# Depthwise convolution of 31 taps: from taps shared by three engines to products of shifted copies on the matrix engine

## The chip, the cores and the metric

The kernel runs on one core of a Trainium2 chip. The metric is the device time of one execution in microseconds (us). The engines are named as in the profile: PE is the matrix engine (PEld its weight loads), DVE the vector engine, ACT the scalar engine, POOL the general engine, SP the engine that issues the DMAs. All engines of the core run at the same time; each takes its own instructions strictly in the order in which they were written down, and semaphores make one wait for another.

## What is computed

The reference is a chain of layers on a sequence of 512 tokens with 1024 features, all in float32. The change touches one of them, the "conformer" layer, and in it one line: a causal convolution over time, for each feature by itself, with 31 taps.

```python
def causal_dwconv(x, w):              # x (1, 512, 1024), w (31, 1024)
    k_w = w.shape[0]
    return lax.conv_general_dilated(
        x, w[:, None, :].astype(x.dtype), window_strides=(1,), padding=[(k_w - 1, 0)],
        dimension_numbers=('NWC', 'WIO', 'NWC'), feature_group_count=x.shape[-1])

def conformer_conv(h, w_in, b_in, dw, dw_b, ln_g, ln_b, w_out, b_out):
    D = h.shape[-1]
    u = h @ w_in + b_in
    u = u[..., :D] * jax.nn.sigmoid(u[..., D:])
    u = causal_dwconv(u, dw) + dw_b
    u = jax.nn.silu(layernorm(u, ln_g, ln_b))
    return u @ w_out + b_out
```

So the output at time t is the sum over the lags d = 0 to 30 of the input at t - d times the tap of lag d of that feature. Before this layer stands a feed-forward layer (`ffn`, layer 0), behind it a cross attention (`xattn`, layer 1), whose keys and values are worked out from another input, `mem`, of 256 tokens.

## The kernel before

**Layout.** Features lie on the 128 partitions, in 8 chunks j = 0 to 7; the 512 tokens lie along the free dimension. A tile of one chunk is 128x512 in float32.

**Dense products.** `linear` (L222) takes weight tiles of 128 input rows by 1024 values. Each is loaded from DRAM by a DMA that SP issues into one of two raw buffers (`wr`, L51), and is split into a high part (ACT, L63) and a low part (DVE or POOL, L64), for which there are three buffers each. `acc3` (L212) then makes each product of three fast matmuls (L218 to L220). The weights `kv_k1` and `kv_v1` are not split: they are used from the raw buffer, in one plain float32 matmul (L216). A plain float32 matmul is two records of PE in the trace, each with a weight load of its own.

**The conformer layer (L576).** For each chunk j, `lin([j])` makes two output tiles (the gate and the value, 48 fast matmuls together); `evict` (L621) scales them by the norm's factor on DVE, takes the sigmoid on ACT and writes `us[j]` on DVE (L629). Then `conv(j)` (L590) writes `ys[j]`, and `add(j)` (L618) adds the mean over the features, by a plain float32 product, into a PSUM bank `sums` that collects over all chunks. The loop at L636 issues, for each j: `lin([j + 2])`, one eighth of the attention's keys (`next(keys)`, 8 plain float32 matmuls of 256 columns), `conv(j)`, `add(j - 1)`. `memory` (called at L634) prepares the input for the keys. Behind the loop come the last `add`, the layer norm over the features, which can start only when all eight chunks are in `sums`, and the attention's values (L216 again), put into the gaps of the layer norm by `fill`.

**`conv(j)` before.** The 31 lags are cut in three, by the table `TAPS`. The first `npe` lags (25 over all chunks) are products on PE with a diagonal matrix `dg`, which ACT makes (L598, L599). The last 8 to 14 lags (100 in all) are a multiplication on ACT into `cq` (L605, L608) and an addition on POOL (L609). The lags between them (123 in all) are fused multiply-adds on DVE into `ys[j]` (L611, L613). Two more DVE instructions (L614, L615) join the three sums and the bias.

**The order.** The program is written down with its dependencies, and a planner puts the instructions of each engine in an order: it goes through a model of the run, takes what is ready there, and among that what was written first. Buffers that are used in turn are waited for in the same way. The order that comes out is fixed; at run time an instruction that has to wait holds up all behind it on its engine, the DMAs on SP included.

Of the kernel before, what the change touches and what calls it, by code (L numbers as in the profile page):

```python
# [8 lines left out]
F32 = mybir.dt.float32  # L9
F32R = mybir.dt.float32r  # L10
AF = mybir.ActivationFunctionType
ALU = mybir.AluOpType
# [3 lines left out]
P = 128  # L16
T = 512
D = 1024
KD = D // P
# [76 lines left out]
class Net:  # L96
# [472 lines left out]

            self.linear(f"xattn_w_o{l}", KD, list(range(KD)), lambda k: o[k], out)  # L570


    KEYS = (0, 1, 2, 3, 4, 5, 6, 7)
    TAPS = [(2, 14), (1, 12), (1, 14), (1, 14), (1, 14), (1, 12), (6, 12), (12, 8)]

    def conformer(self, l, g_next):  # L576

        nc = self.nc
        self.logs = False
        rs = self.norm_done(1e-6)  # L580
        xs, side = self.xs, self.side
        ys, us, gate = {}, {}, {}
        ctx = ExitStack()
        mp = ctx.enter_context(self.tc.tile_pool(name=f"mn{l}", bufs=1, reuse_waits="tile"))
        tp = ctx.enter_context(self.tc.tile_pool(name="cz", bufs=1, reuse_waits="tile"))
        mean = tp.tile([P, P], F32, name="mean")
        nc.gpsimd.memset(mean, 1.0 / D)
        sums = self.aux()

        def conv(j):  # L590
            u = us[j]
            w = lambda d: self.vec("conv_dw", 31 * j + 30 - d)
            y = self.slot(1 - side, "h", j)
            npe, npo = self.TAPS[j]
            ps = self.aux()
            for d in range(npe):
                dg = tp.tile([P, P], F32, tag="dg", bufs=3, name=self.nm("dg"))
                nc.scalar.activation(out=dg, in_=self.ident, func=AF.Copy, scale=w(d))  # L598
                nc.tensor.matmul(ps[:, d:], lhsT=dg, rhs=u[:, : T - d], start=(d == 0), stop=(d == npe - 1), skip_group_check=True)  # L599
            z = tp.tile([P, T], F32, tag="cz", bufs=5, name=self.nm("cz"))  # L600
            d0 = 31 - npo
            for d in range(d0, 31):
                if d == d0:
                    nc.gpsimd.memset(z[:, :d], 0.0)
                    nc.scalar.activation(out=z[:, d:], in_=u[:, : T - d], func=AF.Copy, scale=w(d))  # L605
                else:
                    q = tp.tile([P, T], F32, tag="cq", bufs=2, name=self.nm("cq"))
                    nc.scalar.activation(out=q[:, d:], in_=u[:, : T - d], func=AF.Copy, scale=w(d))  # L608
                    nc.gpsimd.tensor_tensor(out=z[:, d:], in0=z[:, d:], in1=q[:, d:], op=ALU.add)  # L609
            nc.vector.memset(y[:, :npe], 0.0)  # L610
            nc.vector.tensor_scalar(out=y[:, npe:], in0=u[:, : T - npe], scalar1=w(npe), scalar2=None, op0=ALU.mult)  # L611
            for d in range(npe + 1, d0):
                nc.vector.scalar_tensor_tensor(out=y[:, d:], in0=u[:, : T - d], scalar=w(d), in1=y[:, d:], op0=ALU.mult, op1=ALU.add)  # L613
            nc.vector.tensor_tensor(out=y, in0=y, in1=z, op=ALU.add)  # L614
            nc.vector.scalar_tensor_tensor(out=y, in0=ps, scalar=self.vec("conv_dw_b", j), in1=y, op0=ALU.add, op1=ALU.add)  # L615
            ys[j] = y

        def add(j, x):  # L618
            self.last_sum = nc.tensor.matmul(sums, lhsT=mean, rhs=x, start=(j == 0), stop=(j == KD - 1))

        def evict(m, ps):  # L621
            u = self.t512("u", 3)
            nc.vector.tensor_tensor(out=u, in0=ps, in1=rs, op=ALU.mult)  # L623
            if m >= KD:
                nc.scalar.activation(out=u, in_=u, func=AF.Sigmoid, bias=self.vec("conv_b_in", m))
                gate[m - KD] = u
            else:
                us[m] = self.slot(1 - side, "l", m)
                nc.vector.scalar_tensor_tensor(out=us[m], in0=u, scalar=self.vec("conv_b_in", m), in1=gate.pop(m), op0=ALU.add, op1=ALU.mult)  # L629

        keys = self.memory_keys(l)
        lin = lambda js: self.linear("conv_w_in", KD, [m for j in js for m in (KD + j, j)], lambda k: xs[k], evict, group=2)
        lin([0])
        self.memory(mp, False)  # L634
        lin([1])
        for j in range(KD):  # L636
            if j < 6:
                lin([j + 2])
            if j in self.KEYS:
                km = next(keys)  # L640
            conv(j)
            if j:
                add(j - 1, ys[j - 1])
        for km in keys:
            pass
        values = self.memory_values(l)
        vm = next(values)

        def fill(n, after):
            with self.tc.issue_after(after.ins):  # L650
                for _ in range(n):
                    next(values)

        fill(FILL[0], self.last_sum)
        add(KD - 1, ys[KD - 1])
        fill(FILL[1], self.last_sum)
        for j in range(KD):
            nc.vector.tensor_tensor(out=ys[j], in0=ys[j], in1=sums, op=ALU.subtract)
        ps = self.aux()
        for j in range(KD):  # L660
            s = self.t512("sq", 2) if j else self.t512("acc", 1)
            nc.scalar.activation(out=s, in_=ys[j], func=AF.Square)
            if j:
                nc.vector.tensor_tensor(out=acc, in0=acc, in1=s, op=ALU.add)
            else:
                acc = s
        for b in range(4):
            last = nc.tensor.matmul(ps[:, b : b + 1], lhsT=acc[:, b * P : (b + 1) * P], rhs=self.ones[:, 0:1], start=True, stop=True)
        fill(FILL[2], last)
        v = self.small(4, "rq")  # L670
        nc.vector.tensor_scalar(out=v, in0=ps[:, :4], scalar1=1.0 / D, scalar2=1e-5, op0=ALU.mult, op1=ALU.add)
        r = self.small(4, "rq")
        self.rsqrt(r, v, 4)
        b = self.bcast_tokens(r)
        fill(FILL[3], self.last_bcast)
        ctx.close()
        zs, done = [], []
        for j in range(KD):
            y = ys[j]
            with self.tc.issue_after(done[-2]) if j > 1 else nullcontext():  # L680
                nc.vector.tensor_tensor(out=y, in0=y, in1=b, op=ALU.mult)
            self.last_silu = nc.scalar.activation(out=y, in_=y, func=AF.Silu, scale=self.vec("conv_ln_g", j), bias=self.vec("conv_ln_b", j)).ins
            hi, lo = self.pair(side, j)
            done.append(self.split(hi, lo, y).ins)
            zs.append((hi, lo))
        self.next_norm(g_next, 1 - side)

        def out(m, ps):
            nc.vector.scalar_tensor_tensor(out=self.x[m], in0=ps, scalar=self.vec("conv_b_out", m), in1=self.x[m], op0=ALU.add, op1=ALU.add)
            self.norm_chunk(m)  # L690

        self.linear("conv_w_out", KD, list(range(KD)), lambda k: zs[k], out)
        return km, vm
# [888 lines left out]
def lay_w(w):  # L1582
    k, m = w.shape
    return w.reshape(k // P, P, m // P, P).transpose(2, 1, 0, 3)


def lay_n(w):

    k, m = w.shape
    return w.reshape(k // 256, 2, P, m // 512, 512).transpose(3, 0, 2, 1, 4).reshape(-1, P, 2, 512)  # L1590
# [113 lines left out]
def by_feature(x):  # L1704
    return x.T.reshape(KD, P, -1).transpose(1, 0, 2)


def arrays(a):

    vl = vec_list(a)  # L1710
    out = {"x": by_feature(a["x"][0]), "mem": by_feature(a["mem"][0]), "vecs": np.concatenate([v for _, v in vl], axis=1)}
    out.update(rw_arrays(a))
    out.update(hy_arrays(a))
    for l in range(2):
        kv = a["xattn_w_kv"][l]
        out[f"kv_k{l}"], out[f"kv_v{l}"] = lay_w(kv[:, :D]), lay_n(kv[:, D:])
        out[f"xattn_w_q{l}"], out[f"xattn_w_o{l}"] = lay_w(a["xattn_w_q"][l]), lay_w(a["xattn_w_o"][l])
        out[f"ffn_w_in{l}"], out[f"ffn_w_out{l}"] = lay_w(a["ffn_w_in"][l]), lay_w(a["ffn_w_out"][l])
    out["conv_w_in"], out["conv_w_out"] = lay_w(a["conv_w_in"][0]), lay_w(a["conv_w_out"][0])
    out["ffn_w_in2"], out["ffn_w_out2"] = lay_w(a["w_up_2"][0]), lay_w(a["w_down_2"][0])  # L1720
    at, n = {}, 0
    for name, v in vl:
        at[name] = n
        n += v.shape[1]
    return out, at
# [35 lines left out]
```

## Time and profile before

| | us |
|---|---|
| median of 3 runs | 2729.18 |
| lowest and highest of them | 2726.78, 2729.96 |
| the profiled execution | 2736.97 |
| its span in the trace | 2735.3 |
| PE busy in the span | 2577.6 |
| DVE busy | 1631.0 |
| ACT busy | 1133.3 |
| POOL busy | 494.1 |

Busy times are shares of the whole span, over stages with different limits. The granted clock (PEclk) is a share of PE's full speed of 2.4 GHz; 0.50 is its lower level, 1.2 GHz, and a mean between the two says how much of a stretch ran at either. The ends of matmuls are modelled, so that neighbours overlap in the records: the distance from start to start is the price of one, and a row of x records that lasts L, where one lasts l, has a distance of (L - l) / (x - 1).

### The profile page before, as it was taken

Reading aid. Unit: us, or ns where it says so; the run is one execution under the profiler, and the core shown is the slowest. Engines: PE = TensorE matmul, PEld = TensorE weight load, DVE = VectorE, ACT = ScalarE, POOL = GpSimd, SP = SyncE. Lnnn points to the kernel's source line nnn. Section 1 sums busy time; section 2 is a strip of 40 time slices with the busy share of each in tenths; the row PEclk is TensorE's granted clock in tenths of the full one; section 3 lists DMA queues with packets and bytes.
Section 4 is the critical chain, followed back from the end, with each engine's and each line's share of the span. In section 5 each row is a group of like instructions: output and inputs, shape, how many; then the busy total and the mean of one; then the engine's idle time right before and its main releaser. Section 6 shows DMA issues by size and latency. Waiting matters only on the chain.

```text
span 2735.3 us, 33003 instructions
## 1 busy us (share of the span) xinstructions
PE 2577.6 (94%) x12974; PEld 2010.9 (74%) x12974; DVE 1631.0 (60%) x2283; ACT 1133.3 (41%) x1826; POOL 494.1 (18%) x446
## 2 busy tenths in 40 slices
PE   6998889899999999776999999999999999999998
PEld 5666668687888888653577888887777567888886
DVE  7674876656677634999655677634324445655522
ACT  6854355434444423543534444323223434433321
POOL 3047433330000011776101000001010000100000
PEclk9997669999999999888999999999989899999999
DMA  3211001331222333210321222322211103322232
GB/s 107 70 61 50 2 24 41 121 104 50 93 93 93 92 98 97 69 62 23 118 91 49 96 95 93 90 89 77 78 55 62 47 32 93 100 95 98 91 92 80
DMA packets 63307, 209.80 MB, mean 77 GB/s; under 512 B 7164, under 2 KB 9485, under 8 KB 63151
## 3 DMA queue, kind: packets, MB, share of 16 engines
q1 hardware_dynamic: 63150, 207.68, 23.6%
q8 instruction: 102, 1.67, 0.3%
q14 instruction: 55, 0.44, 0.1%
HBM read 205.56 MB, written 2.10 MB: 76 GB/s over the span
## 4 chain that ended last, share of the span: by engine, by line
PE 80%; DVE 13%; ACT 2%; POOL 2%; issue 2%; DMA 1%; DVEq 0%; POOLq 0%; ACTq 0%; SPq 0%
PE mm L218 23%; PE mm L220 23%; PE mm L219 23%; DVE bh L613 4%; PE mm L1000 1%; PE aux L321 1%; POOL inv L1316 1%; PE mm L216 1%; POOL inv L1315 1%; PE mm L1367 1%; DVE wl L64 1%; PE aux L980 1%; DVE u L1155 0%; DVE h L1285 0%; DVE h L246 0%
## 5 line engine op out<-in xcount | busy, mean ns | idle before, releaser
L63 ACT ACTIVATE wh<-wr 128x1024 fp32r<-128x1024 f32 (+5 forms) x382 | 388.1, 1019 | 755.1 <-PE mm L219 608.3
L64 DVE TENSOR_TENSOR wl<-wr,wh 128x1024 fp32r<-128x1024 f32 (+3 forms) x341 | 405.8, 1191 | 259.0 <-ACT wh L63 256.6
L218 PE MATMUL mm<-ah,wh 128*128 128x512 f32 x1088 | 435.6, 401 | 11.4 <-DVE u L623 8.3
L219 PE MATMUL mm<-al,wh 128*128 128x512 f32 x1088 | 433.7, 399 | 2.4 <-DVE al L246 2.4
L220 PE MATMUL mm<-ah,wl 128*128 128x512 f32 x1088 | 432.1, 399 | 3.0 <-DVE wl L64 2.8
L218 PE MATMUL mm<-bh,wh 128*128 128x512 f32 (+1 forms) x1000 | 400.0, 401 | 0.0
L219 PE MATMUL mm<-bl,wh 128*128 128x512 f32 (+1 forms) x1000 | 398.8, 399 | 0.0
L220 PE MATMUL mm<-bh,wl 128*128 128x512 f32 (+1 forms) x1000 | 397.0, 399 | 0.0
L269 POOL TENSOR_TENSOR acc<-acc,sq 128x512 f32<-128x512 f32 x55 | 87.3, 1588 | 1005.7 <-ACT sq L268 1005.3
L218 PEld LDWEIGHTS mm<-ah,wh 128*128 128x128 f32 x1088 | 206.5, 190 | 66.0 <-issue 9.8
L220 PEld LDWEIGHTS mm<-ah,wl 128*128 128x128 f32 x1088 | 206.6, 190 | 54.5 <-DVE wl L64 5.6
L219 PEld LDWEIGHTS mm<-al,wh 128*128 128x128 f32 x1088 | 206.2, 189 | 52.5 <-DVE al L246 3.0
L218 PEld LDWEIGHTS mm<-bh,wh 128*128 128x128 f32 (+1 forms) x1000 | 188.6, 189 | 49.8 <-issue 4.0
L220 PEld LDWEIGHTS mm<-bh,wl 128*128 128x128 f32 (+1 forms) x1000 | 188.7, 189 | 48.0 <-issue 1.7
L219 PEld LDWEIGHTS mm<-bl,wh 128*128 128x128 f32 (+1 forms) x1000 | 188.6, 189 | 47.8 <-issue 3.5
L64 POOL TENSOR_TENSOR wl<-wr,wh 128x1024 fp32r<-128x1024 f32 (+2 forms) x41 | 98.2, 2398 | 581.5 <-ACT wh L63 580.0
L381 DVE TENSOR_TENSOR u<-mm,rs 128x512 f32<-128x512 f32 x132 | 90.9, 691 | 177.3 <-PE mm L220 177.3
L609 POOL TENSOR_TENSOR cz<-cz,cq 128x492 f32<-128x492 f32 (+12 forms) x92 | 143.6, 1563 | 70.4 <-ACT cq L608 65.3
L613 DVE SCALAR_TENSOR_TENSOR bh<-bl,vecs,bh 128x505 f32<-128x505 f32 (+18 forms) x115 | 133.8, 1198 | 0.4
L366 DVE TENSOR_TENSOR x<-x,mm 128x512 f32<-128x512 f32 x56 | 38.5, 687 | 140.3 <-PE mm L220 140.2
L218 PE MATMUL mm<-mh,wh 128*128 128x512 f32 (+1 forms) x224 | 88.6, 418 | 5.2 <-ACT mh L245 3.9
L219 PE MATMUL mm<-ml,wh 128*128 128x512 f32 (+1 forms) x224 | 91.5, 409 | 1.7 <-DVE ml L246 1.7
(499 smaller groups left out, 4273.6 us busy)
## 6 DMA issues: line engine op xcount, KB each, us to landing
wr<-ffn_w_in SPq DMA_DIRECT2D x132, 512.0 KB, 3.3
wr<-ffn_w_out SPq DMA_DIRECT2D x48, 448.0 KB, 3.3
wr<-ffn_w_out SPq DMA_DIRECT2D x24, 512.0 KB, 3.5
wr<-hy_g SPq DMA_DIRECT2D x20, 512.0 KB, 3.3
wr<-kv_k SPq DMA_DIRECT2D x16, 512.0 KB, 3.4
wr<-kv_v SPq DMA_DIRECT2D x16, 512.0 KB, 3.4
wr<-xattn_w_q SPq DMA_DIRECT2D x16, 512.0 KB, 3.3
wr<-xattn_w_o SPq DMA_DIRECT2D x16, 512.0 KB, 3.3
```

What stands on the lines that cost most here:

```text
L63: self.last_hi = self.nc.scalar.activation(out=hi[:r, :c], in_=t[:r, :c], func=AF.Copy).ins
L64: (self.nc.gpsimd if i in W_POOL else self.nc.vector).tensor_tensor(out=lo[:r, :c], in0=t[:r, :c], in1=f32(hi[:r, :c]), op=ALU.subtract)
L216: self.last_mm = mm(out, lhsT=w[0], rhs=x[0], start=first, stop=last).ins
L218: mm(out, lhsT=w[0], rhs=x[0], start=first, stop=False)
L219: mm(out, lhsT=w[0], rhs=x[1], start=False, stop=False)
L220: mm(out, lhsT=w[1], rhs=x[0], start=False, stop=last)
L269: nc.gpsimd.tensor_tensor(out=self.sq, in0=self.sq, in1=s, op=ALU.add)
L321: self.last_bcast = self.nc.tensor.matmul(ps[:, b * P : (b + 1) * P], lhsT=col[:, b : b + 1].to_broadcast([P, P]), rhs=self.ident, start=T ...
L366: self.nc.vector.tensor_tensor(out=self.x[m], in0=self.x[m], in1=ps, op=ALU.add)
L381: nc.vector.tensor_tensor(out=u, in0=ps, in1=rs, op=ALU.mult)
L609: nc.gpsimd.tensor_tensor(out=z[:, d:], in0=z[:, d:], in1=q[:, d:], op=ALU.add)
L613: nc.vector.scalar_tensor_tensor(out=y[:, d:], in0=u[:, : T - d], scalar=w(d), in1=y[:, d:], op0=ALU.mult, op1=ALU.add)
```

## The change

The lags are written as d = 4e + i, with e = 0 to 7 and i = 0 to 3 (lag 31 has a tap of zero). For each chunk, `spread(j)` makes a tile `t` of 128 partitions x 4 x 512: for each of the four groups g of 32 features, the four blocks of 32 partitions hold that group's `us[j]` shifted by i = 0, 1, 2, 3 tokens. This takes 16 DMAs of 32 partitions x 2 KB each, from on-chip memory to on-chip memory, issued by SP; POOL sets the first three columns to zero. `spread` also makes `w`, 32 matrices of 128x32, one for each g and e, by one POOL instruction over 1024 values a partition: the taps of the four lags 4e to 4e + 3 stand on the diagonals of four 32x32 blocks. The taps come by one more DMA at the layer's start; `place` is the pattern of ones of those diagonals, made by four small DVE instructions.

`conv(j)` is then 32 plain float32 matmuls with 128 rows and 32 columns of weights and 512 - 4e columns of data. Those of group g write to partitions 32g to 32g + 31 of one PSUM bank, so they use the g-th quarter of the array's columns. Their order is e outside, g inside. One ACT instruction adds the bias and writes `ys[j]`. The parts on DVE, on ACT and POOL, and the diagonal matrices, are gone. `spread(0)` is written behind `memory`, and `spread(j + 1)` at the start of the loop's turn j; `t` and `w` have two buffers each.

```diff
-    TAPS = [(2, 14), (1, 12), (1, 14), (1, 14), (1, 14), (1, 12), (6, 12), (12, 8)]
...
+        taps = tp.tile([P, KD, 32], F32, name="taps")
+        nc.sync.dma_start(out=taps, in_=self.a["conv_taps"])
+        place = tp.tile([P, 32], F32, name="place")
+        nc.vector.tensor_copy(place, self.ident[:, :32])
+        for i in range(1, 4):
+            nc.vector.tensor_tensor(out=place, in0=place, in1=self.ident[:, 32 * i : 32 * i + 32], op=ALU.add)
         sums = self.aux()
 
+        def spread(j):
+
+            t = tp.tile([P, 4, T], F32, tag="cu", bufs=2, name=self.nm("cu"))
+            nc.gpsimd.memset(t[:, :, :3], 0.0)
+            for i in range(4):
+                for g in range(4):
+                    nc.sync.dma_start(out=t[32 * i : 32 * i + 32, g, i:], in_=us[j][32 * g : 32 * g + 32, : T - i])
+            w = tp.tile([P, 32, 32], F32, tag="cw", bufs=2, name=self.nm("cw"))
+            nc.gpsimd.tensor_tensor(out=w, in0=place.rearrange("p (a c) -> p a c", a=1).to_broadcast([P, 32, 32]),
+                                    in1=taps[:, j].rearrange("p (a c) -> p a c", c=1).to_broadcast([P, 32, 32]), op=ALU.mult)
+            return t, w
+
         def conv(j):
...
+            t, w = spreads.pop(j)
             ps = self.aux()
...
+            for e in range(8):
+                for g in range(4):
+                    nc.tensor.matmul(ps[32 * g : 32 * g + 32, 4 * e :], lhsT=w[:, 8 * g + e], rhs=t[:, g, : T - 4 * e], start=(e == 0), stop=(e == 7),
+                                     skip_group_check=True)
+            ys[j] = self.slot(1 - side, "h", j)
+            nc.scalar.activation(out=ys[j], in_=ps, func=AF.Identity, bias=self.vec("conv_dw_b", j))
...
+        spreads = {}
         lin([0])
         self.memory(mp, False)
+        spreads[0] = spread(0)
         lin([1])
         for j in range(KD):
+            if j < 7:
+                spreads[j + 1] = spread(j + 1)
             if j < 6:
                 lin([j + 2])
             if j in self.KEYS:
...
+
+    dw = np.concatenate([a["conv_dw"][0][::-1], np.zeros((1, D), np.float32)])
+    out["conv_taps"] = dw.reshape(8, 4, KD, 4, 32).transpose(1, 4, 2, 3, 0).reshape(P, KD, 32)
```

The lines left out of `conv` are the whole of its old body, which the code above shows.

## Rows read from the trace of the kernel before

**Rows 1.** The page, its first part: busy time of each engine over the span.
```profile
PE 2577.6 (94%) x12974; PEld 2010.9 (74%) x12974; DVE 1631.0 (60%) x2283; ACT 1133.3 (41%) x1826; POOL 494.1 (18%) x446
```

**Rows 2.** Busy times by stretch of the conformer layer, its fill, and the whole layer.
```profile
core 0: us, PE busy (x) PEld busy (x) DVE busy (x) ACT busy (x) POOL busy (x), PEclk, DMA share, GB/s
...
1107.90:1141.20 33.30, 22.48 (x97) 18.26 (x98) 32.08 (x33) 20.05 (x31) 26.87 (x20) 0.87 0.20 67
...
1209.10:1249.20 40.10, 26.57 (x87) 19.31 (x86) 40.10 (x37) 15.06 (x23) 30.49 (x19) 0.79 0.11 40
...
1299.00:1329.60 30.60, 29.75 (x81) 13.43 (x79) 20.95 (x38) 19.48 (x29) 0.00 (x0) 1.00 0.36 121
1069.50:1299.00 229.50, 176.93 (x632) 125.22 (x632) 212.44 (x208) 109.20 (x181) 145.19 (x96) 0.87 0.17 56
```

**Rows 3.** Groups of instructions by line, 1069.5 to 1299 us, costliest first.
```profile
line engine op names shapes xcount | busy us, mean ns | idle before us <-releasers
L609 POOL TENSOR_TENSOR cz<-cz,cq 128x492 f32<-128x492 f32 (+12 forms) x92 | 143.6, 1563 | 70.4 <-ACT cq L608 65.3
L613 DVE SCALAR_TENSOR_TENSOR bh<-bl,vecs,bh 128x505 f32<-128x505 f32 (+18 forms) x115 | 133.8, 1198 | 0.4
L608 ACT ACTIVATE cq<-bl,vecs 128x492 f32<-128x492 f32 (+12 forms) x92 | 62.9, 695 | 37.6 <-POOL cz L609 37.3
...
L619 PE MATMUL aux<-bh,mean 128*128 128x512 f32 x16 | 12.9, 901 | 21.6 <-DVE bh L615 21.6
...
L436 PE MATMUL aux<-ones,sq 128*128 128x1 f32 x32 | 4.2, 238 | 1.6 <-ACT sq L433 1.6
```

**Rows 4.** The chain that ended last, 1069.5 to 1299 us, shares by line.
```profile
by line: DVE bh L613 47.2%; issue 9.9%; DVE wl L64 5.6%; DVE h L246 3.9%; DVE u L623 3.9%; DVE bl L629 3.8%; DVE bh L611 3.3%; DVE bh L614 2.3%; PE mm L220 2.2%; PE mm L218 2.2%; PE mm L219 2.1%; DMA wr<-conv_w_in 2.1%; PE aux L599 1.8%; DV
```

**Rows 5.** Timeline of PE (start us, length us, line, xrecords): dense product, key, values.
```profile
1117.71 0.48 PE L218 MATMUL mm<-ah,wh 128*128 128x512 f32 x1
...
1128.99 3.62 PE L216 MATMUL mm<-mn,wr 128*128 128x256 f32 x16
...
1298.88 10.79 PE L216 MATMUL mm<-wr,mn 128*128 128x512 f32 x24
...
1310.32 3.68 PE L216 MATMUL mm<-wr,mn 128*128 128x512 f32 x8
```

**Rows 6.** Timeline of PE: matmuls that alternate between quarters, then halves, of the columns.
```profile
267.24 1.06 PE L1296 MATMUL aux<-zr,h 64*32 64x32 f32 x60 [0.27 <-DVE h L1285]
...
467.17 0.64 PE L1448 MATMUL chain<-am,uv 128*64 128x64 f32 x16
467.74 0.38 PE L218 MATMUL mm<-mnh,wh 128*128 128x256 f32 x1
```

**Rows 7.** Busy times and granted clock of those two, columns as in rows 2.
```profile
267.24:268.20 0.96, 0.96 (x60) 0.93 (x60) 0.96 (x2) 0.78 (x3) 0.64 (x1) 0.50 0.00 0
467.17:467.74 0.57, 0.57 (x22) 0.50 (x19) 0.28 (x1) 0.55 (x2) 0.00 (x0) 1.00 0.02 7
```

**Rows 8.** Line 1296's instructions: xcount, shortest/median/longest ns, first and last start us.
```profile
L1296 PE MATMUL aux<-zr,h x512: 185/237/260, 151.9 to 308.8; 64*32 64x32 f32 x171
```

**Rows 9.** Line 1448's instructions, in the same form.
```profile
L1448 PEld LDWEIGHTS chain<-am,uv x256: 132/139/233, 262.2 to 479.9; 128*64 128x64 f32 x128
L1448 PE MATMUL chain<-am,uv x256: 221/223/370, 262.2 to 480.0; 128*64 128x64 f32 x128
```

**Rows 10.** Line 1016's weight loads of 32 columns, in the same form.
```profile
L1016 PEld LDWEIGHTS aux<-ident,rp x16: 93/96/97, 2066.7 to 2212.0; 128*32 128x32 f32 x16
```

**Rows 11.** The costliest groups on the page: POOL over 128x1024.
```profile
L64 POOL TENSOR_TENSOR wl<-wr,wh 128x1024 fp32r<-128x1024 f32 (+2 forms) x41 | 98.2, 2398 | 581.5 <-ACT wh L63 580.0
```

**Rows 12.** Timeline of SP at the kernel's start: eight issues in a row.
```profile
0.80 3.71 SPq L1116 DMA_DIRECT2D vv<-x  x8
```

**Rows 13.** DMA issues: xcount, KB each, median us from issue to landing.
```profile
u<-mem SPq DMA_DIRECT2D x16, 128.0 KB, 2.4
```

**Rows 14.** What SP waited for, 1050 to 1340 us: total us, times, longest.
```profile
SPq L51 <- DVE wl L64: 114.2, 18, 12.9
```

More of the change, by code (lines that the diff above doesn't have):

```diff
@@ L590, in conv @@
         def conv(j):
[L591 to L594, printed above, removed]
+            t, w = spreads.pop(j)
             ps = self.aux()
[L596 to L615, printed above, removed]
@@ L616, in conv @@
-            ys[j] = y
+            for e in range(8):
[4 more added lines that the diff above has]
+            nc.scalar.activation(out=ys[j], in_=ps, func=AF.Identity, bias=self.vec("conv_dw_b", j))
         def add(j, x):
```

## The prediction

> **What bounds the kernel now.** Read the page's busy times first: PE is busy for 94% of the span [rows 1], so over the whole run PE sets the time, and an engine beside it counts only where PE waits for it. Then the busy times by stretch find such a place. In the conformer layer, from 1107.9 us on, DVE is full (32.08 of 33.30 us, 40.10 of 40.10) while PE is busy for two thirds of each stretch, at a granted clock of 0.87 and 0.79; over the whole layer, 229.5 us, DVE is busy for 212.44 and the clock is 0.87 [rows 2]. PE waits, and because it waits it is partly given its lower clock. Behind the layer's last mean, in the fill, PE is full again (29.75 of 30.60 at 1.00 [rows 2]). The groups by line say what DVE does there: 115 multiply-adds of the convolution, 133.8 us; POOL's share of the taps is 143.6 us beside it and ACT's 62.9, and PE's idle time before the mean products, 21.6 us, ends on DVE's last line of the convolution [rows 3]. The chain of waits agrees: 47.2% of this layer is that one DVE line [rows 4]. So the layer, from its first dense product at 1069.5 to its last mean at 1299, is bound by the convolution on DVE. If that leaves DVE, the layer is as long as PE's own work.
>
> **PE's work without the convolution, all at full clock.** One chunk's dense products run from 1117.71 to 1128.99, 11.28 us [rows 5]; eight are 90.2. One key is 16 records in 3.62 us, of which the last one's overhang is some 0.2 [rows 5]; eight are 28. A plain float32 record of 512 columns costs (10.79 - 3.68) / 16 = 0.444 us, by the rows of 24 and of 8 such records [rows 5]; the eight means, 16 records, are 7.1. The small products (the sums for the norms, 4.2 us of them on L436 [rows 3], and the broadcasts) I put at 7. Together 132 us.
>
> **The new products.** 8 chunks x 8 values of e x 4 groups x 2 records = 512 records, of 498 columns on average (512 - 4e), at 0.444 x 498/512 = 0.432 us each if one ran behind the other: 221 us, more than is there to gain. All hangs on how many of the four column groups run side by side. No row shows four groups over 128 rows at 512 columns, so I bound it. The first row: a record of 256 columns costs 3.4/16 = 0.213 us at full clock, 0.83 ns a column, so one of 64 columns costs 53 ns alone. In L1448, which alternates between two column halves with 128 rows, 16 records take (0.64 - 0.22) / 15 = 28 ns each at a clock of 1.00 [rows 6, 7, 9]: 1.9 side by side, about all that two halves allow. The second: L1296 goes through four column quarters with 64 rows each at a clock of 0.50, where 32 columns cost 53 ns alone; 60 records take (1.06 - 0.24) / 59 = 13.9 ns each [rows 6 to 8]: 3.8 side by side. From this I take four. Then the convolution is 512 x 0.432 / 4 = 55.3 us, 6.9 a chunk. Ends: 55 (four), 110 (two, the least that L1448 leaves for 128 rows), 221 (one).
>
> A rule of the Trainium skill speaks against it. "TensorE: Matmul & The Clock Gate", Part 3, says that a weight load overlaps running matmuls only when its row group differs; here all four groups use all rows. By that rule the loads would stand bare between the products, and the sum would be that of rival 3. In L1448 both halves use all 128 rows too, and a load lasts 139 ns where records follow each other every 28 [rows 6, 9]: there the loads overlap, and the rule does not hold as it is put.
>
> **What goes.** The 25 taps on PE, 123 instructions on DVE for the lags between, 16 that join the sums, and 100 each on ACT and POOL. DVE keeps the evictions and the weight splits: 212 less 134 for L613 and some 20 for the others is 58 us in a layer of some 190, so DVE is not next.
>
> **What comes beside PE.** POOL: 8 x 2.4 us for `w` (L64's POOL form over the same 1024 values [rows 11]) in place of 145 us; PE's work hides it. ACT: 8 evictions of about 0.7 us (L608's mean [rows 3]) in place of 100 multiplications; free but for the last, which the last mean waits for: 1 us, where a DVE instruction stood. SP: 16 issues a chunk. Eight issues in a row took 3.71 us [rows 12], so 16 are 7.4, and with a landing of 2.4 us (the row of 128 KB [rows 13]; these have 64) a chunk's copies are there some 10 us after its buffer comes free. They are written a whole turn (11.3 + 3.5 + 6.9 + 0.9 = 22.6 us of PE) ahead of their use. In the last two turns, which have no dense product, `spread(7)` may start when `conv(5)` ends and is needed after key 6, `conv(6)`, a mean and key 7: 14.8 us, still more than 10. But SP is one queue: a copy that waits for `conv(j - 1)` holds up the weight loads written behind it, and with them ACT's and DVE's splits. SP stands waiting for much of this layer already (114.2 us on buffers that DVE's splits set free, up to 12.9 us at once [rows 14]), so the queue has room: 128 issues are 59 us of 190. Each turn needs three weight loads, and the next turn's are due only 22 us on. I take a cost of 2 us at the start, where `spread(0)`, `spread(1)` and the eight loads of `mem` come together; ends: 0, and 4 us in each of seven turns, 28.
>
> On PE itself there are 16 changes between the whole array and quarters. L1448's 16 records at 28 ns end their starts at 467.59, and L218 starts at 467.74 [rows 6], 0.15 us later, which I take for one change less a step, 0.12 each: 1.9 us. The groups start staggered, and the first product of a chunk waits for several semaphores: 0.3 us a chunk, 2.4, an assumption. With the last eviction, 1, and the start, 2, that is 7 us. Bounds: 0 to 12, apart from SP's end above.
>
> **The sum.** 132 + 55 + 7 = 194 us in place of 229.5: 35 us less. Nothing behind the layer's last mean gives or takes: there PE is already full [rows 2]. The sum is made on the profiled execution (2736.97), which is 7.8 us above the median of 2729.18; I take the difference from the median: 2694 us.
>
> **Rivals.**
> 1. *Two side by side.* Four streams of float32 over all 128 rows at full clock appear in no row. If the array is fed only two, or is given its lower clock in these stretches (as L1296's was, 0.50 [rows 7]), a chunk costs 13.8 us and the layer 132 + 110 + 7 = 249: 20 us more than before, 2749. It decides from 11.3 us a chunk on ((229.5 - 132 - 7) / 8), 2.4 side by side. For it: 128 rows are shown only with two halves. Against: 3.8 of four in L1296.
> 2. *SP holds up the weights.* PE stalls 4 us in seven turns: 28 of the 35 are lost, 2722. For it: one queue with a fixed order. Against: the loads are due late.
> 3. *The weight loads are not hidden.* 512 loads of 96 ns (L1016's 128x32 [rows 10]) stand between the products: 49 us more, so 14 slower than before, 2743. L1448 speaks against it.
> 4. *No column group beside another*: the change doesn't do what it says. 132 + 221 + 7 = 360: 131 us more, 2860. L1296 and L1448 both speak against it.
>
> **How the numbers follow.** My forecast has 0.61 (its own range 2684 to 2708: the bounds of the 7 us, and the same again for PE's other work), rival 2 has 0.17 (2708 to 2726), rival 1 0.13, rival 3 0.05, rival 4 0.03; 0.01 is left for a gain over 45 us, for which there is no work of PE to remove. The range 2683 to 2744 leaves out rivals 1 and 4 and little else. A measurement here tells 0.2%, 5.5 us, from no change. Faster by more: the forecast and nearly all of rival 2, 0.76. Within: the last of rival 2, 0.03. Slower: 0.21.
>
> **What would show it.** In the changed profile: (a) the 64 records of a chunk's convolution take 6.9 us, the granted clock 1.00; 13.8 is rival 1, 13 with loads between the products rival 3. (b) The stretch from the first dense product to the last mean is about 194 us with PE full; gaps of PE that end on ACT's or DVE's splits or on a weight DMA are rival 2. (c) DVE's busy time falls by 150 us and POOL's by 125. The prediction is wrong if (a) holds and the stretch is not shorter by some 30 us, or if a stage behind it becomes longer by what this one saves.

## The result and the profile after

The changed kernel takes 2689.15 us (median; 2685.6 to 2691.29) beside 2729.57 us of the kernel before on the same chip: a ratio of 0.9847, 95% interval 0.9834 to 0.9860, that is 38 to 45 us less. The prediction was 2694 us, its range 2683 to 2744; the measured time lies 5 us below the forecast and within the range. The profiled execution is 2691.29 us, its span 2688.5.

The first part of the page of the changed kernel, beside [rows 1]:

```profile
PE 2581.6 (96%) x13436; PEld 2000.3 (74%) x13436; DVE 1463.5 (54%) x2140; ACT 1067.4 (40%) x1709; POOL 368.3 (14%) x362
```

PE's busy time has hardly moved, 2577.6 to 2581.6 us, in a span 47 us shorter: PE has more products to make, and what went is time in which it waited or ran at its lower clock. DVE's fell by 167 us and POOL's by 126.

Busy times by stretch of the changed kernel, with the columns of [rows 2]; the layer now runs from 1069.3 us, its first dense product, to 1255.4, and the last row is the fill behind it:

```profile
core 0: us, PE busy (x) PEld busy (x) DVE busy (x) ACT busy (x) POOL busy (x), PEclk, DMA share, GB/s
1069.30:1107.90 38.60, 38.60 (x188) 32.00 (x187) 13.53 (x23) 16.66 (x28) 5.63 (x4) 1.00 0.40 116
1107.90:1163.30 55.40, 55.40 (x350) 34.18 (x348) 16.51 (x27) 15.07 (x19) 3.95 (x4) 1.00 0.50 143
1163.30:1255.40 92.10, 92.10 (x562) 54.45 (x560) 15.20 (x23) 11.41 (x18) 8.97 (x8) 1.00 0.36 98
1069.30:1255.40 186.10, 186.10 (x1094) 120.63 (x1093) 45.24 (x73) 43.14 (x64) 18.55 (x16) 1.00 0.41 115
1255.40:1286.30 30.90, 29.89 (x81) 13.35 (x79) 20.95 (x37) 19.47 (x29) 0.00 (x0) 1.00 0.37 119
```

This is the reading to learn: PE is busy for 186.10 of 186.10 us at a granted clock of 1.00, where it was 176.93 of 229.50 at 0.87 [rows 2]. DVE fell from 212 to 45 us, POOL from 145 to 19. The layer is 43.4 us shorter, and the fill behind it has kept its length (30.6 before, 30.9 now). The span fell by 46.8; the profiled execution of before, 2736.97 us, was itself 7.8 above its median, so I give the 3 us by which the span fell further than the layer no cause in the change.

One turn of the loop on PE's timeline (start, length, line, records):

```profile
1140.73 1.12 PE L619 MATMUL aux<-bh,mean 128*128 128x512 f32 x2
1141.29 0.80 PE L218 MATMUL mm<-ah,wh 128*128 128x512 f32 x1
...
1152.89 3.62 PE L216 MATMUL mm<-mn,wr 128*128 128x256 f32 x16
1156.43 6.89 PE L613 MATMUL aux<-cu,cw 128*32 128x512 f32 x64
1163.25 1.12 PE L619 MATMUL aux<-bh,mean 128*128 128x512 f32 x2
1163.81 0.80 PE L218 MATMUL mm<-ah,wh 128*128 128x512 f32 x1
```

From L218 to L218 a turn is 22.52 us with no gap: 11.60 dense, 3.54 key, 6.82 convolution, 0.56 mean. In the convolution 64 records start within 6.82 us, 0.107 us each, a quarter of the 0.43 that one of them costs alone. The groups by line of that line, weight loads and products, with count, shortest, median and longest ns:

```profile
L613 PEld LDWEIGHTS aux<-cu,cw x512: 106/110/110, 1117.4 to 1252.6; 128*32 128x32 f32 x171
L613 PE MATMUL aux<-cu,cw x512: 569/580/617, 1117.4 to 1253.0; 128*32 128x508 f32 x22, 128*32 128x496 f32 x22, 128*32 128x484 f32 x22, 128*32 128x512 f32 x21
```

A load of 110 ns and a start every 107 ns on average leave no room for loads that stand between the products: they run beside them. One set of four loads on PEld's timeline, 0.46 us into the convolution, just where its second four products start:

```profile
1156.89 0.13 PEld L613 LDWEIGHTS aux<-cu,cw 128*32 128x32 f32 x4 [0.30 <-issue]
```

The four loads overlap one another too, 0.13 us for all of them. SP's timeline in the same turn:

```profile
1140.75 0.33 SPq L51 DMA_DIRECT2D wr<-conv_w_in  x1
1141.17 10.03 SPq L601 DMA_DIRECT2D cu<-bl  x16
1151.30 0.53 SPq L51 DMA_DIRECT2D wr<-conv_w_in  x1
1156.53 0.33 SPq L51 DMA_DIRECT2D wr<-kv_k  x1
1157.45 7.64 SPq L51 DMA_DIRECT2D wr<-conv_w_in  x2
```

The landing of the copies, from the list of DMA issues (count, KB each, median us):

```profile
cu<-bl SPq DMA_DIRECT2D x32, 64.0 KB, 2.1
```

The 16 copies of a chunk take 10.0 us to issue and 2 more to land, 12 in place of my 10. The weight loads issued behind them are still in time: PE has no gap in this turn.

### The profile page after: what moved, and what is told of

It reads as the page before. It is cut to its first block, busy times and chain, and to the rows that moved or that the text cites. A ratio compares the mean times of both kernels' runs of the same rounds, so it can differ in the third digit from the quotient of the medians.

```text
span 2688.5 us, 33718 instructions
## 1 busy us (share of the span) xinstructions
PE 2581.6 (96%) x13436; PEld 2000.3 (74%) x13436; DVE 1463.5 (54%) x2140; ACT 1067.4 (40%) x1709; POOL 368.3 (14%) x362
## 4 chain that ended last, share of the span: by engine, by line
PE 88%; DVE 7%; ACT 2%; POOL 2%; issue 1%; DMA 0%; DVEq 0%; POOLq 0%; ACTq 0%
PE mm L218 24%; PE mm L220 24%; PE mm L219 24%; PE aux L613 2%; PE mm L216 2%; PE aux L321 1%; PE mm L1004 1%; PE mm L1371 1%; POOL inv L1320 1%; POOL inv L1319 1%; PE aux L984 1%; DVE u L1159 1%; DVE h L1289 0%; DVE ml L246 0%; PE aux L1000 0%
## 5 line engine op out<-in xcount | busy, mean ns | idle before, releaser
L218 PE MATMUL mm<-ah,wh 128*128 128x512 f32 x1088 | 432.8, 398 | 0.9 <-ACT wh L63 0.9
L218 PE MATMUL mm<-bh,wh 128*128 128x512 f32 (+1 forms) x1000 | 399.7, 401 | 0.0
L218 PEld LDWEIGHTS mm<-ah,wh 128*128 128x128 f32 x1088 | 204.7, 188 | 54.2 <-ACT wh L63 3.7
L218 PEld LDWEIGHTS mm<-bh,wh 128*128 128x128 f32 (+1 forms) x1000 | 188.6, 189 | 49.9 <-issue 3.9
L218 PE MATMUL mm<-mh,wh 128*128 128x512 f32 (+1 forms) x224 | 87.7, 413 | 5.2 <-ACT mh L245 3.7
L220 PE MATMUL mm<-mh,wl 128*128 128x512 f32 (+1 forms) x224 | 90.1, 405 | 1.3 <-DVE wl L64 1.3
L395 ACT ACTIVATE uy<-uy 128x512 f32<-128x512 f32 x66 | 41.6, 632 | 122.5 <-DVE uy L393 122.4
```

The lines of the kernel that those rows point to most:

```text
L218: mm(out, lhsT=w[0], rhs=x[0], start=first, stop=False)
L220: mm(out, lhsT=w[1], rhs=x[0], start=False, stop=last)
```

## The experiments

**One group alone.** Is the convolution's price that of one column group, or does each group pay a share?

```diff
             for e in range(8):
-                for g in range(4):
-                    nc.tensor.matmul(ps[32 * g : 32 * g + 32, 4 * e :], lhsT=w[:, 8 * g + e], rhs=t[:, g, : T - 4 * e], start=(e == 0), stop=(e == 7),
+                for g in range(4 if e == 0 else 1):
+                    nc.tensor.matmul(ps[32 * g : 32 * g + 32, 4 * e :], lhsT=w[:, 8 * g + e], rhs=t[:, g, : T - 4 * e], start=(e == 0), stop=(e == 7 or g > 0),
```

> The changed kernel with the products of column groups 1 to 3 left out for e = 1 to 7 (28 of 31 lags of three quarters of the features are missing); group 0 keeps all eight values of e. 22 of a chunk's 64 records stay. Theory (four groups run side by side, each at the price that a record has alone): group 0 alone is the length of the chunk, 16 x 0.43 = 6.9 us, so nothing is saved: the layer stays at 187 us, the time at 2689 (+-5). Rival (the four groups share something, so that a record costs 0.108 us in turn): a chunk falls to 22 x 0.108 = 2.4 us, the layer to 151, the time to 2653.

Measured: 2687.5 us (one run). PE's timeline:

```profile
1152.62 6.87 PE L613 MATMUL aux<-cu,cw 128*32 128x512 f32 x22
```

22 records take 6.87 us where 64 took 6.89; the layer is 186.2 us. Leaving out 42 of 64 records saves nothing, so the other three groups are free beside the first. The rival's 2.4 us is out.

**Halves in place of quarters.** Two shifted copies of 64 features, 128x64 weights, e = 0 to 15. The copies, the weights and the taps are laid out to match; those lines are left out here.

```diff
-            for e in range(8):
-                for g in range(4):
-                    nc.tensor.matmul(ps[32 * g : 32 * g + 32, 4 * e :], lhsT=w[:, 8 * g + e], rhs=t[:, g, : T - 4 * e], start=(e == 0), stop=(e == 7),
+            for e in range(16):
+                for g in range(2):
+                    nc.tensor.matmul(ps[64 * g : 64 * g + 64, 2 * e :], lhsT=w[:, 16 * g + e], rhs=t[:, g, : T - 2 * e], start=(e == 0), stop=(e == 15),
```

> The changed kernel with two copies and two column groups in place of four: 64 features by two shifts on the 128 partitions, lags d = 2e + i with e = 0 to 15, 128x64 weights, 4 copies of 64 partitions a chunk; again 64 records of about 497 columns a chunk, and one buffer for the weights. Theory (time is records x 0.43 over the number of column groups): 64 x 0.43 / 2 = 13.8 us a chunk, the layer 187 + 55 = 242, the time 2744, slower than before the change. Rival (what counts is the number of records, whatever their columns): 6.9 us a chunk, 2689.

Measured: 2747.97 us (one run), against 2731.67 before: slower than before, as expected. A chunk on PE's timeline:

```profile
1170.69 13.55 PE L613 MATMUL aux<-cu,cw 128*64 128x512 f32 x64
```

The layer's busy times:

```profile
1070.30:1312.90 242.60, 239.74 (x1094) 142.90 (x1093) 46.43 (x71) 42.87 (x64) 31.44 (x15) 1.00 0.25 71
```

The same number of records costs 13.55 us, twice 6.89, and the layer is 242.6 us (242 expected). With DVE just as free as in the changed kernel, this one loses: the gain needs the quarters, not only the move away from DVE. It is also what my first rival, two side by side, would have looked like.

**The groups one behind another.** Does the order of the 64 records matter?

```diff
-            for e in range(8):
-                for g in range(4):
+            for g in range(4):
+                for e in range(8):
```

> The changed kernel with the two loops exchanged: g outside, e inside, so that the 16 records of one column group stand behind each other; the same 512 records. Theory (records are handed out in the order in which they are written, and one that finds its columns taken holds up those behind it): the groups run one behind the other but for an overlap at the three borders, 16 x 4 x 0.43 - 3 x 0.4 = 26.4 us a chunk in place of 6.9, the layer 187 + 156 = 343, the time 2845. Rival (PE looks past a record that has to wait): 6.9 us a chunk, 2689.

Measured: 2811.5 us (one run); a chunk:

```profile
1186.19 22.11 PE L613 MATMUL aux<-cu,cw 128*32 128x512 f32 x64
```

Between the two theories, near the first: 22.1 us, where I had 26.4 and the rival 6.9. How the difference comes about is to be seen in the records started in four pieces of one chunk (busy times by stretch of that line alone; the numbers in brackets count the records that fall into a piece):

```profile
1148.44:1153.50 5.06, 5.04 (x12) 1.35 (x13) 1.00 0.71 233
1153.50:1154.87 1.37, 1.37 (x9) 0.51 (x8) 1.00 0.02 9
1154.87:1158.58 3.71, 3.71 (x12) 0.96 (x9) 1.00 0.44 141
1158.58:1159.95 1.37, 1.37 (x9) 0.51 (x8) 1.00 0.00 0
```

In the first and the third piece the records come one by one, some 0.42 us apart (the counts take in one that still runs from the piece before); in the other two eight or nine fall into 1.37 us: the last four of a group with the first four of the next. So at each of three borders four records are saved, not one: 52 steps of 0.42 us are 21.8. In this program's order the 16 records of a group do stand behind each other; in the trace the first record of the next group, known by its 512 columns, starts with the 13th of the group before, ahead of three that were written before it, and not sooner, though its own columns are free. So PE is not strictly bound to its order: it starts a record some four places ahead of one that has to wait, but no farther. For 16 records of one group that is far too little, and the loop order, g inside, carries 122 us.

**One buffer for the copies.** What hides the copies, and what does SP's queue cost when the cover is thin?

```diff
-            t = tp.tile([P, 4, T], F32, tag="cu", bufs=2, name=self.nm("cu"))
+            t = tp.tile([P, 4, T], F32, tag="cu", bufs=1, name=self.nm("cu"))
```

> The changed kernel with one buffer for the shifted copies in place of two, so that the copies for a chunk start when the product before it ends. Theory (copies take some 10 us from then, and only PE's work between the two products has to cover them): the turns with dense products cover them (11.3 + 3.5 + 0.9 us); in the last two turns only a key and a mean stand there, 4.5 us, so PE waits some 5.5 us twice: the layer 198, the time 2700. Rival (SP's queue is what counts, copies that wait hold up weight loads in each turn): 4 us and more in each of seven turns, the layer 215 or longer, 2717 to 2730. If copies were there at once: 2689.

Measured: 2722.78 us, 0.9968 of the kernel before (0.9956 to 0.9979). Most of the gain is gone, as the rival said, but not by its mechanism. PE's waits for the copies:

```profile
PE aux L613 <- DMA cu<-bl: 9.4, 2, 6.0
```

They are 9.4 us, in the last two turns, near the 11 of the theory. In the turns before PE has no gap, at the dense products or elsewhere, so no weight load comes too late, though SP stands waiting for the convolution before:

```profile
SPq L601 <- PE aux L613: 54.5, 7, 14.1
```

What the theory missed is PE's own work, on its timeline in a turn:

```profile
1136.87 0.40 PE L218 MATMUL mm<-ah,wh 128*128 128x512 f32 x1
1137.19 1.04 PE L613 MATMUL aux<-cu,cw 128*32 128x512 f32 x2
1138.17 0.50 PE L219 MATMUL mm<-al,wh 128*128 128x512 f32 x1
1138.51 0.40 PE L220 MATMUL mm<-ah,wl 128*128 128x512 f32 x1
1138.83 1.04 PE L613 MATMUL aux<-cu,cw 128*32 128x512 f32 x2
1139.81 0.50 PE L218 MATMUL mm<-ah,wh 128*128 128x512 f32 x1
1140.15 0.40 PE L219 MATMUL mm<-al,wh 128*128 128x512 f32 x1
1140.47 1.90 PE L613 MATMUL aux<-cu,cw 128*32 128x512 f32 x16
```

The planner, which sees some copies land before others, has drawn the first product of single groups forward, between dense products. Such a pair of records stands alone in the array and costs 1 us, where its share among four groups is 0.2, and the group that is not drawn forward still takes its full 6.9. Three pairs a turn (the third stands at 1133.30) make a turn 25.8 us long in place of 22.5. In the last two turns PE, after its wait, also gets the lower clock (the stretches of the last wait and of the two convolutions):

```profile
1255.00:1267.00 12.00, 11.44 (x64) 5.66 (x64) 0.00 (x0) 0.00 (x0) 0.00 (x0) 0.72 0.26 71
1267.80:1274.90 7.10, 1.12 (x3) 0.32 (x3) 0.00 (x0) 0.00 (x0) 0.00 (x0) 0.79 0.45 101
1274.90:1285.50 10.60, 10.07 (x64) 5.00 (x64) 0.00 (x0) 0.00 (x0) 0.00 (x0) 0.82 0.14 32
```

The sum: 9.4 us of waits, some 14 for thirteen lone pairs in five turns (1.1 each, from the longer turn), and 9 for the two convolutions of 12.0 and 10.6 us instead of 6.9; together 32 of the layer's 35 (221 - 186). The rest is in small gaps behind those two.

**The kernel before without DVE's taps.** Was DVE alone what held it? The convolution on PE, ACT and POOL stays as it was; 107 multiply-adds on DVE are missing.

```diff
-            for d in range(npe + 1, d0):
+            for d in range(npe + 1, npe + 2):
```

> The kernel before, with 107 of DVE's 115 multiply-adds of the convolution left out (one a chunk stays; the lags between are missing from the result); the taps on PE, ACT and POOL stay. Theory (DVE alone made the layer 229.5 us long; PE's own work with the old 25 taps is 132 + 22 = 154): what ends last is then PE, or POOL's 92 additions, 144 us or less, behind a start of some 25 us: the layer 165 to 180 us, the time 2666 to 2681. Rival (PE's lower clock and the chain through ACT and POOL hold the layer): 200 us or more, 2701 or more.

Measured: 2672.95 us (one run). The layer's busy times:

```profile
1067.40:1237.00 169.60, 155.95 (x632) 114.90 (x631) 93.05 (x101) 108.55 (x181) 127.64 (x96) 0.99 0.23 75
```

The layer is 169.6 us in place of 229.5, PE busy for 155.95 (154 by the sum) at a clock of 0.99. Taking DVE's share away is enough to make the layer nearly as short as PE's own work and to give PE its clock back; of the 13.7 us in which PE is idle, 6.3 end on ACT's diagonal matrices. The chain through ACT and POOL, whose taps are still there, did not set the 229.5 us by its own length.

That does not clear POOL. In the trace of the kernel before, the same multiply-add on DVE has two prices. First DVE and POOL where POOL works, then DVE where POOL does not (POOL's last row has its idle time before it):

```profile
1226.82 4.96 DVE L613 SCALAR_TENSOR_TENSOR bh<-bl,vecs,bh 128x506 f32<-128x506 f32 x3
1225.89 7.00 POOL L609 TENSOR_TENSOR cz<-cz,cq 128x483 f32<-128x483 f32 x4
1217.81 3.35 DVE L613 SCALAR_TENSOR_TENSOR bh<-bl,vecs,bh 128x509 f32<-128x509 f32 x5
1221.74 2.45 POOL L609 TENSOR_TENSOR cz<-cz,cq 128x485 f32<-128x485 f32 x1 [4.39 <-ACT cq L608]
```

Beside POOL's additions one takes some 1.65 us, without them 0.67. At 0.73 us, the mean length of the 40 that run while POOL is idle, the 115 of them would be 84 us of DVE in place of 133.8; so some 50 us of DVE's full queue go with POOL's share of the taps (an estimate from these rows). No run leaves out POOL's taps alone, so how much of the gain that by itself would have brought is not shown. The changed kernel takes away both.

**Taps given back to DVE.** If the layer is the longer of PE's and DVE's work, the best split lies between the two kernels: fewer values of e on PE, the highest lags on DVE (here for 16 lags on PE).

```diff
-            for e in range(8):
+            for e in range(4):
...
-            ys[j] = self.slot(1 - side, "h", j)
-            nc.scalar.activation(out=ys[j], in_=ps, func=AF.Identity, bias=self.vec("conv_dw_b", j))
+            y = ys[j] = self.slot(1 - side, "h", j)
+            v = lambda d: self.vec("conv_dw", 31 * j + 30 - d)
+            nc.vector.memset(y[:, :16], 0.0)
+            nc.vector.tensor_scalar(out=y[:, 16:], in0=us[j][:, : T - 16], scalar1=v(16), scalar2=None, op0=ALU.mult)
+            for d in range(17, 31):
+                nc.vector.scalar_tensor_tensor(out=y[:, d:], in0=us[j][:, : T - d], scalar=v(d), in1=y[:, d:], op0=ALU.mult, op1=ALU.add)
+            nc.vector.scalar_tensor_tensor(out=y, in0=ps, scalar=self.vec("conv_dw_b", j), in1=y, op0=ALU.add, op1=ALU.add)
```

> The changed kernel with e = 0 to 4 on PE (lags 0 to 19) and the lags 20 to 30 on DVE, which has been idle for three quarters of the layer: a multiplication, ten multiply-adds and one that joins PSUM and bias, in place of ACT's eviction. Theory (the layer is as long as the longest of PE's own work and DVE's own work): PE 187 - 8 x 3 x 0.86 = 166 us; DVE 45 + 8 x (11 x 0.73 + 1) = 117, or 159 if a multiply-add costs 1.2 us as it did before beside POOL. So the layer is 166 us, the time 2668. Rival (PE waits for DVE's last instruction before each mean, as in the kernel before): 175 or more, 2677 or more.

> The same with e = 0 to 3 on PE and the lags 16 to 30 on DVE. Theory: PE 187 - 8 x 4 x 0.86 = 159.5 us; DVE 45 + 8 x (15 x 0.73 + 1) = 141 us, below it: the layer 160, the time 2662. If a multiply-add costs 1.2 us, DVE is 45 + 8 x 19 = 197 and bounds: 2699.

> The same with e = 0 to 2 on PE and the lags 12 to 30 on DVE. Theory: PE 152.6 us, DVE 45 + 8 x (19 x 0.73 + 1) = 164 us, with a start at which it has no input, some 20 us in: DVE bounds, the layer 165 to 185, the time 2667 to 2687, slower than with e = 0 to 3. If DVE's work does not bound, 153 us and 2655.

Measured: 2676.55 us with 20 lags on PE, 2665.5 with 16, 2671.77 with 12; the ratios to the kernel before are 0.9799 (0.9774 to 0.9824), 0.9755 (0.9727 to 0.9782) and 0.9779 (0.9756 to 0.9802). All three intervals lie below that of the change under study (0.9834 to 0.9860), so each split beats both kernels; but they overlap one another, so that 16 is the best of the three rests on the medians and on the layer's length. The layer's busy times, first with 20 lags on PE:

```profile
1068.10:1240.50 172.40, 169.06 (x901) 115.13 (x901) 114.50 (x169) 37.96 (x56) 17.69 (x16) 1.00 0.44 124
```

With 16:

```profile
1070.50:1237.60 167.10, 163.57 (x838) 113.18 (x837) 135.71 (x201) 37.93 (x56) 18.45 (x16) 1.00 0.45 128
```

With 12:

```profile
1069.90:1239.10 169.20, 157.31 (x774) 111.57 (x774) 152.74 (x233) 37.89 (x56) 22.52 (x16) 0.98 0.45 126
```

PE's busy time falls from row to row, by 5.5 and 6.3 us for one e less (6.9 expected), and DVE's rises, by 21 and 17. With 16 lags PE is still full but for 3.5 us. With 12 PE is idle for 12 us, and its waits in the layer's last 50 us end on DVE's joining instruction L621, as they ended on L615 before:

```profile
PEld aux L624 <- DVE bh L621: 10.4, 3, 7.5
PE aux L624 <- DVE bh L621: 7.7, 3, 6.7
```

So the turning point stands where the theory had it, as far as the medians tell. The times are 4 to 9 us above its two figures of 2668 and 2662: the layer is 172.4 and 167.1 in place of 166 and 159.5. Some 3.5 us of each are gaps of PE, which end on DVE, here with 16 lags (L307 belongs to the norm of the attention's input):

```profile
PE aux L321 <- DVE mcol L307: 2.7, 1, 2.7
PE aux L624 <- DVE bh L621: 0.9, 1, 0.9
```

The rest of 2.9 and 4.1 us goes for the most part to lone pairs of convolution records, as in the experiment with one buffer: two stand in the trace with 20 lags and three with 16, at some 1.1 us each.

The split with 16 lags also bears on POOL: DVE has 112 multiply-adds in this layer there, where the kernel before had 115, but they take 87.6 us in place of 133.8, and PE is nearly full beside them. POOL, busy for 18.45 us of the layer there in place of 145, is seldom beside them:

```profile
L620 DVE SCALAR_TENSOR_TENSOR bh<-bl,vecs,bh 128x483 f32<-128x483 f32 (+12 forms) x112 | 87.6, 792 | 2.2
```

## Why the prediction was right

- *DVE bound the layer* [rows 2 to 4]. Shown by the kernel before without DVE's taps: 169.6 us for the layer, and the clock back at 0.99. What the prediction did not see in its own rows is that a part of DVE's time hangs on POOL: 1198 ns for a multiply-add on average, where one takes 0.67 us while POOL is idle. DVE's other work became shorter too (L629 has a mean of 750 ns after the change, 1548 before): the layer keeps 45 us of DVE, where the prediction had 58.
- *PE's work without the convolution, 132 us.* The layer is 186.1 us with PE full; less 8 x 6.82 of convolution, 131.5.
- *Four side by side, 6.9 us a chunk* [rows 6 to 9]. 6.89 measured. One group alone costs the same, halves twice as much. The rivals of two groups, of loads that are not hidden and of no overlap are all out. But the step from the rows to "four" was longer than it reads: L1296 takes its four column quarters in two row halves of 64 (two quarters with the upper rows, two with the lower, by the code of that line), so neither it nor L1448 had shown more than two groups side by side over the same rows. That four do is shown only by the changed kernel. The sentence of the Trainium skill ("TensorE: Matmul & The Clock Gate", Part 3) that loads overlap only in another row group does not hold here, taken by itself: all groups use all rows, and the loads are hidden.
- *Copies hidden by a turn's lead; SP costs 2 us.* Right in what it says of the time: PE's busy time is the whole stretch, so they cost nothing. My 7.4 us for 16 issues was too small, 10.0 measured. The rival that SP holds up the weights did not come even with one buffer, where 9.4 us of the loss were waits for the copies themselves and the rest was PE's own.
- *7 us for changes of shape, staggered starts and waits.* This is the term that was mis-sized: there is no gap to be seen. With nothing here the sum is 187, against 186.1 measured. The changes of shape do show, at about 0.1 us each, near the 0.12 assumed: from the last key record to the first quarter 0.31 us in place of 0.22. A turn is 22.52 us with them, where the prediction's prices give 22.6 without: the dense products take 11.60 us behind a mean in place of 11.28, and a mean 0.56 in place of 0.89. The 0.3 us a chunk for staggered starts and waits had no row behind it, and no gap of PE shows it; nor does one show the 2 us of SP at the start. So the layer came out 8 us shorter than the 194 of the sum, and the time only 5 below 2694. The other 3 stay open; the 229.5 us that the gain was counted from are those of an execution 7.8 us above its median.
- *The range of the forecast itself, 2684 to 2708.* Its bounds are turned round: 7 us with ends of 0 and 12, taken twice, are 14 less and 10 more, 2680 to 2704. The measured time lies in either.
- *Nothing behind the layer gives or takes.* The fill is 30.9 us (30.6 before).

## What to carry to other kernels

Where the page of the profile calls PE the bound of the whole, look by stretch for one in which PE is not full and its granted clock is below 1.00; there the engine that is full is the one to relieve, and the gain is at most the layer's length less PE's own work at full clock. Before work is split among engines, compare the price of one instruction with and without its neighbour at work: here a multiply-add on DVE cost 0.67 us alone and 1.65 beside POOL. Small products that use a quarter of the array's columns cost a quarter only if records of the four groups stand next to each other in PE's order: one group alone costs as much as four. Once one engine is relieved, hand it back work until its busy time comes near that of the one that took it.

## What was not expected of the hardware

- PE starts a record of another column group up to about four records ahead of one that waits for its own columns, so the opening statement that each engine takes its instructions strictly in order holds for PE only up to there; 64 records in blocks of 16 a group took 22.1 us, next to each other 6.9, and one behind another they would take 27 (64 x 0.42).
- A product of one column group that stands alone between dense products costs 1.0 us for its two records, where eight records next to each other in four groups take 0.86.
- A fused multiply-add of DVE over some 500 columns took 1.65 us while POOL added beside it and 0.67 us while POOL was idle, in the same layer of the same trace.
- Issues of copies from on-chip memory to on-chip memory, 64 KB over 32 partitions each, took 0.63 us each in a row of 16 (10.03 us), against 0.46 for the loads at the kernel's start [rows 12].
- Four groups kept PE at its full clock: 1.00 over the whole layer, with 55 us of such products in it.
